# High and low part of x side by side: one 512-column matmul for both in the first feed-forward projections

## The chip, the cores and the metric
The kernel runs on one core of one Trainium2 chip. The metric is the device time of one execution in microseconds (us), the median over runs. TensorE (PE) multiplies, VectorE (DVE) and ScalarE (ACT) work elementwise, GpSimd (POOL) helps, and SyncE (SP) issues most DMAs. Matmul results land in PSUM, which has 8 banks of 512 fp32 values in each of 128 partitions; everything else on the chip lies in SBUF.

## The reference, cut to what matters
A sequence of 256 tokens of width 1024 goes through two blocks in fp32. The first has a mixer, attention over a memory and a feed-forward in each of two layers; the second has two layers of gated feed-forward, attention, gated feed-forward. The two kinds of feed-forward are

```python
def squared_relu_mlp(h, w1, w2):
    a = jax.nn.relu(h @ w1)
    return (a * a) @ w2

def swiglu(x, w_in, w_out):
    gate, up = jnp.split(x @ w_in, 2, axis=-1)
    return (jax.nn.silu(gate) * up) @ w_out
```

with 4096 inner columns in the first (two of them) and 2816 in the second (four of them). `h` is `x` after an RMS norm with a gain.

## The kernel before
Activations lie with the features on the partitions: x is 8 chunks of 128 features by 256 tokens. To keep fp32 accuracy every operand of a large matmul is split into a high part, which TensorE's fast fp32 format holds exactly, and a low part, the rest. A product is then three matmuls (`mm3`, L217 to L219): high weight by high x, low weight by high x, high weight by low x, each with 128x128 weights and 256 columns. The high and low part of x are the tiles `xhi` and `xlo`, written by `prep` (ACT for the high part, DVE for the low one); the gain is applied there, and the norm's factor for each token (`rstd_row`, whose matmul is L448) is applied when a result leaves PSUM.

Weights come in 568 groups of 128x1024. SP loads a group into one of the `raw` tiles, ACT rounds it into `rhi` (L204) and DVE subtracts for `rlo` (L242), each in halves of 512; seven groups are held split (`take`, `pump`, `split`).

A feed-forward loops over jobs. `W1(j)` takes a PSUM bank and two weight groups, runs `projs` (8 k-steps, two outputs of 256 columns side by side in the bank), and evicts the bank: in the gated one `evac_row` multiplies by the norm's factor (DVE L210), ACT applies silu, DVE multiplies, ACT and DVE split the result again. `W2` takes such a result as one chunk of the second projection (`rows`), which accumulates in banks 0 to 3 over the whole loop. `bank()` hands out banks 4 to 7 in turn; the stick stage (`stick_mixer`) hands out all 8.

The order of instructions on each engine is set by a list scheduler of the framework, which orders by priority and its own costs and then puts semaphore waits where one engine uses what another wrote or read. It tracks these dependences by tile. PSUM is eight tiles of one bank.

Attention stages (`even_mixer`, `mem_attention`, `band_mixer`, `stick_mixer`, `shared_kv`, `sink_mixer`) use the same banks: projections of q, k and v, scores, transposes and products, with VectorE and ScalarE between. In the stick stage each pair of heads has four matmuls into a bank A (L1224, L1226) and two into a bank B (L1228), whose sums DVE adds; in the sink stage a q projection is multiplied by the norm's factor and then rotated by a matmul (`rope`, L1245). During the first layer's memory attention, `mem_jobs` projects the memory; some of these jobs run later, as filler.

Of the kernel before, what the change touches and what calls it, by code (L numbers as in the profile page):

```python
# [8 lines left out]
F32 = mybir.dt.float32  # L9
# [92 lines left out]

class Kern:
    def __init__(self, nc, tc, ctx, d):
# [15 lines left out]
        self.xh = R(2048, "xhi")  # L120
        self.xl = R(2048, "xlo")
# [11 lines left out]
        self.psum = [ctx[1].tile([128, 512], F32, name=f"ps{i}") for i in range(8)]  # L133
# [131 lines left out]
    def proj(self, out, spec, xh=None, xl=None):  # L265
        xh = self.xh if xh is None else xh
        xl = self.xl if xl is None else xl
        wh, wl = self.take(spec)
        for k in range(8):
            self.mm3(out, wh[:, k * 128:(k + 1) * 128], wl[:, k * 128:(k + 1) * 128],  # L270
                     xh[:, k * 256:(k + 1) * 256], xl[:, k * 256:(k + 1) * 256], k == 0, k == 7)
        self.done()

    def projs(self, jobs, xh=None, xl=None):

        xh = self.xh if xh is None else xh
        xl = self.xl if xl is None else xl
        ws = [[self.take(spec) for spec in specs] for _, specs in jobs]
        for k in range(8):
            for (ps, _), w in zip(jobs, ws):  # L280
                for o, (wh, wl) in enumerate(w):
                    self.mm3(ps[:, o * 256:(o + 1) * 256], wh[:, k * 128:(k + 1) * 128], wl[:, k * 128:(k + 1) * 128],
                             xh[:, k * 256:(k + 1) * 256], xl[:, k * 256:(k + 1) * 256],
                             k == 0 and o == 0, k == 7 and o == len(w) - 1, skip=True)
        self.done(sum(len(w) for w in ws))

    def proj_toks(self, jobs, name, xh=None, xl=None):
        xh = self.xh if xh is None else xh
        xl = self.xl if xl is None else xl
        ws = [[self.take((name, "tok", c0, h)) for h in range(2)] for _, c0 in jobs]  # L290
        R = lambda z: z.bitcast(F32R)
        for k in range(8):
            for (ps, _), w in zip(jobs, ws):
                wh, wl = (R(z[:, (k % 4) * 256:(k % 4 + 1) * 256]) for z in w[k // 4])
                for t in range(2):
                    ah = R(xh[:, k * 256 + t * 128:k * 256 + (t + 1) * 128])
                    al = R(xl[:, k * 256 + t * 128:k * 256 + (t + 1) * 128])
# [6 lines left out]
    def proj_tok(self, ps, name, c0, xh=None, xl=None):  # L304
        self.proj_toks([(ps, c0)], name, xh, xl)

    def proj_wide(self, pss, name, c0, xh=None, xl=None):

        xh = self.xh if xh is None else xh
        xl = self.xl if xl is None else xl  # L310
        R = lambda z: z.bitcast(F32R)
        for q in range(4):
            wh, wl = self.take((name, "wide", c0, q))
            for k in (2 * q, 2 * q + 1):
                h, l = (R(z[:, (k % 2) * 512:(k % 2 + 1) * 512]) for z in (wh, wl))
                for t in range(2):
                    ah = R(xh[:, k * 256 + t * 128:k * 256 + (t + 1) * 128])
                    al = R(xl[:, k * 256 + t * 128:k * 256 + (t + 1) * 128])
# [34 lines left out]
    def prep(self, c, gain, x=None, xh=None, xl=None):  # L353
        x = self.x if x is None else x
# [146 lines left out]
    def mem_start(self, mem):  # L501
        for b in range(4):
            self.a.dma_start(mem[:, b * 512:(b + 1) * 512], self.d["mem"][:, b * 512:(b + 1) * 512])
        for b in range(4):
            for c in (2 * b, 2 * b + 1):
                self.prep(c, ("mg", 0), mem, self.mh, self.ml)
# [938 lines left out]
```

## Time and profile before

| | us |
|---|---|
| median of 3 runs | 1834.97 (1834.53 to 1837.04) |
| profiled execution, its own time | 1834.19 |
| its span | 1832.5 |
| TensorE busy | 1786.8 |
| VectorE busy | 1242.7 |
| ScalarE busy | 1033.3 |

The profiled execution is 1.7 us longer than its span, which begins with the first and ends with the last instruction. Busy times are sums over a stretch in which the engines overlap. A matmul's duration in a row is longer than the distance to the next matmul's start, since they are pipelined; the distance is what a matmul costs in a stream. TensorE's granted clock is full in nearly all of the span.

### The profile page before, as it was taken

How to read it: one execution, taken by the hardware profiler on the slowest of the kernel's cores; microseconds unless marked ns; L12 is line 12 of the kernel's file. 1: busy time of each engine (PE TensorE's matmuls, PEld its weight loads, DVE VectorE, ACT ScalarE, POOL GpSimd, SP SyncE). 2: the span in 40 equal slices, each digit the busy share in tenths (PEclk: the TensorE clock that was granted, in tenths of full speed). 3: DMA queues.
4: the chain of work that ended last, by engine and by line, in shares of the span. 5: the costliest groups of instructions: out<-in, count | busy, mean ns of one | idle time of the engine just before them, and what ended most of it. 6: DMA issues, size and time to landing. Idle time of an engine off the chain costs nothing.

```text
span 1832.5 us, 35979 instructions
## 1 busy us (share of the span) xinstructions
PE 1786.8 (98%) x14362; PEld 1741.3 (95%) x14362; DVE 1242.7 (68%) x2261; ACT 1033.3 (56%) x2037; POOL 110.3 (6%) x128
## 2 busy tenths in 40 slices
PE   7899999999999989998999999999999999999997
PEld 7889999999999989998999998999999999899997
DVE  7877786557687585557656778766586566876564
ACT  6556565556566465556444667644474455774443
POOL 2320000000000000000000002000010000200000
PEclk9999999999999999999999999999999999999999
DMA  7434445554653435553555553555545555335551
GB/s 272 159 119 137 161 148 198 185 184 156 225 166 139 156 133 189 187 185 137 188 190 176 184 173 127 172 174 188 191 162 187 181 181 174 118 128 188 192 173 35
DMA packets 85624, 307.80 MB, mean 168 GB/s; under 512 B 9680, under 2 KB 10320, under 8 KB 85456
## 3 DMA queue, kind: packets, MB, share of 16 engines
q1 hardware_dynamic: 83952, 300.92, 48.1%
q0 software_dynamic: 640, 3.15, 0.6%
q8 instruction: 112, 1.84, 0.4%
q10 hardware_dynamic: 864, 1.44, 0.2%
q14 instruction: 56, 0.46, 0.1%
HBM read 304.42 MB, written 1.05 MB: 167 GB/s over the span
## 4 chain that ended last, share of the span: by engine, by line
PE 92%; DVE 4%; ACT 2%; issue 1%; POOL 1%; DMA 0%; DVEq 0%; SPq 0%; ACTq 0%
PE ps L217 26%; PE ps L219 26%; PE ps L218 26%; PE ps L319 1%; PE ps L321 1%; PE ps L320 1%; DVE rlo L242 1%; PE ps L300 1%; PE ps L301 1%; PE ps L299 1%; PE ps L912 1%; PE ps L1080 1%; PE ps L930 1%; POOL u L210 1%; PE ps L448 1%
## 5 line engine op out<-in xcount | busy, mean ns | idle before, releaser
L204 ACT CAST rhi<-raw 128x512 fp32r<-128x512 f32 (+1 forms) x1138 | 669.8, 617 | 644.7 <-PE ps L219 609.3
L242 DVE TENSOR_TENSOR rlo<-raw,rhi 128x512 fp32r<-128x512 f32 (+1 forms) x1138 | 760.3, 693 | 342.0 <-ACT rhi L204 336.6
L217 PE MATMUL ps<-xhi,rhi 128*128 128x256 f32 x2560 | 732.5, 286 | 16.4 <-ACT xhi L192 9.5
L219 PE MATMUL ps<-xlo,rhi 128*128 128x256 f32 x2560 | 729.3, 285 | 4.3 <-DVE xlo L213 4.2
L218 PE MATMUL ps<-xhi,rlo 128*128 128x256 f32 x2560 | 729.3, 285 | 0.0
L217 PEld LDWEIGHTS ps<-xhi,rhi 128*128 128x128 f32 x2560 | 492.3, 192 | 18.9 <-ACT xhi L192 10.3
L219 PEld LDWEIGHTS ps<-xlo,rhi 128*128 128x128 f32 x2560 | 491.5, 192 | 6.5 <-DVE xlo L213 6.2
L218 PEld LDWEIGHTS ps<-xhi,rlo 128*128 128x128 f32 x2560 | 492.3, 192 | 0.7 <-DVE rlo L242 0.3
L217 PE MATMUL ps<-u,rhi 128*128 128x256 f32 x1680 | 474.6, 283 | 0.0
L219 PE MATMUL ps<-u,rhi 128*128 128x256 f32 x1680 | 471.8, 281 | 0.0
L218 PE MATMUL ps<-u,rlo 128*128 128x256 f32 x1680 | 471.4, 281 | 0.0
L217 PEld LDWEIGHTS ps<-u,rhi 128*128 128x128 f32 x1680 | 317.1, 189 | 0.9 <-issue 0.7
L218 PEld LDWEIGHTS ps<-u,rlo 128*128 128x128 f32 x1680 | 317.1, 189 | 0.4 <-issue 0.2
L219 PEld LDWEIGHTS ps<-u,rhi 128*128 128x128 f32 x1680 | 316.4, 188 | 0.7 <-DVE u L207 0.7
L210 DVE TENSOR_TENSOR u<-ps,rst 128x512 f32<-128x512 f32 (+1 forms) x129 | 84.1, 656 | 110.6 <-PE ps L219 110.2
L210 POOL TENSOR_TENSOR ssum<-ssum,sqb 128x512 f32<-128x512 f32 x26 | 38.0, 1461 | 1283.9 <-ACT sqb L192 1282.3
L192 ACT ACTIVATE u<-u 128x256 f32<-128x256 f32 (+3 forms) x158 | 86.2, 548 | 34.6 <-PE ps L702 17.1
L207 DVE TENSOR_TENSOR u<-u,u 128x256 fp32r<-128x256 f32 (+2 forms) x128 | 66.7, 521 | 10.2 <-ACT u L204 8.5
L204 ACT CAST u<-u 128x256 fp32r<-128x256 f32 (+2 forms) x128 | 61.9, 484 | 11.1 <-POOL u L1177 7.1
L213 DVE SCALAR_TENSOR_TENSOR xlo<-xres,gain,xhi 128x256 fp32r<-128x256 f32 x96 | 57.0, 620 | 3.1 <-ACT xhi L192 3.1
L192 ACT ACTIVATE xhi<-xres,gain 128x256 fp32r<-128x256 f32 x96 | 43.4, 501 | 26.4 <-DVE xres L210 19.7
L210 DVE TENSOR_TENSOR u<-u,u 128x256 f32<-128x256 f32 (+2 forms) x107 | 51.2, 481 | 0.6 <-ACT u L192 0.5
(170 smaller groups left out, 1261.2 us busy)
## 6 DMA issues: line engine op xcount, KB each, us to landing
raw<-w SPq DMA_DIRECT2D x567, 512.0 KB, 3.9
u<-bias POOLq DMA_DIRECT2D x8, 384.0 KB, 3.9
xres<-x SPq DMA_DIRECT2D x4, 256.0 KB, 5.3
u<-mem ACTq DMA_DIRECT2D x4, 256.0 KB, 4.0
raw<-w SPq DMA_DIRECT2D x2, 256.0 KB, 4.6
u<-tabs SPq DMA_DIRECT2D x1, 512.0 KB, 5.0
out<-u SPq DMA_DIRECT2D x2, 256.0 KB, 2.6
u<-masks SPq DMA_DIRECT2D x1, 256.0 KB, 6.4
```

The costliest lines, as they stand in the source:

```text
L192: i = self.a.activation(out, in_, func, scale=scale, **kw)
L204: return self.a.copy(out.bitcast(F32R), in_)
L207: return self.v.tensor_tensor(out.bitcast(F32R), in_, hi, ALU.subtract)
L210: return (eng or self.v).tensor_tensor(out, a, b, op)
L213: return self.v.scalar_tensor_tensor(out, a, s, b, op0, op1)
L217: self.pe.matmul(out, R(wh), R(xh), start=start, stop=False, skip_group_check=skip)
L218: self.pe.matmul(out, R(wl), R(xh), start=False, stop=False, skip_group_check=skip)
L219: self.pe.matmul(out, R(wh), R(xl), start=False, stop=stop, skip_group_check=skip)
L242: b = self.v.tensor_tensor(l[:, c].bitcast(F32R), r[:, c], h[:, c], ALU.subtract)
L299: self.pe.matmul(o, ah, wh, start=k == 0 and t == 0, stop=False, skip_group_check=True)
L300: self.pe.matmul(o, ah, wl, start=False, stop=False, skip_group_check=True)
L301: self.pe.matmul(o, al, wh, start=False, stop=k == 7 and t == 1, skip_group_check=True)
```

## The change
`xhi` and `xlo` become one tile `xpair`, in which each chunk has its 256 high columns and then its 256 low columns. `Pair` gives a chunk's both, high or low part; `Apart` gives the same for operands that stay in two tiles (the memory and the shared keys and values). All projections read x through them.

In W1 of both feed-forwards `projs2` takes the place of `projs`: for each k-step and output one matmul of the high weight with all 512 columns, into a whole bank, and one of the low weight with the 256 high columns, into the second half of the bank. So a job's two outputs take two banks, and each bank holds two partial sums. `halves` has ScalarE copy the second halves to SBUF and VectorE add the first ones; what followed then reads SBUF. PSUM is declared as four tiles of two banks; `psum[i]` are views of their halves, and `pair_bank` hands out the third and the fourth tile in turn. The row of sums in the feed-forwards uses bank 3.

```diff
+class Pair:
+    def both(self, c):
+        return self.tile[:, c * 512:(c + 1) * 512]
+    def h(self, c):
+        return self.tile[:, c * 512:c * 512 + 256]
+    def l(self, c):
+        return self.tile[:, c * 512 + 256:(c + 1) * 512]
...
-        self.xh = R(2048, "xhi")
-        self.xl = R(2048, "xlo")
+        self.xp = Pair(R(4112, "xpair")[:, 12:4108])
...
-        self.psum = [ctx[1].tile([128, 512], F32, name=f"ps{i}") for i in range(8)]
+        self.psum2 = [ctx[1].tile([128, 1024], F32, name=f"ps{i}") for i in range(4)]
+        self.psum = [self.psum2[i // 2][:, i % 2 * 512:(i % 2 + 1) * 512] for i in range(8)]
...
+    def pair_bank(self):
+        self.nbank += 3 - self.nbank % 2
+        return self.psum2[2 + self.nbank // 2 % 2]
+
+    def projs2(self, jobs):
+        ws = [[self.take(spec) for spec in specs] for _, specs in jobs]
+        R = lambda z: z.bitcast(F32R)
+        for k in range(8):
+            c = slice(k * 128, (k + 1) * 128)
+            for (ps, _), w in zip(jobs, ws):
+                for o, (wh, wl) in enumerate(w):
+                    self.pe.matmul(ps[:, o * 512:(o + 1) * 512], R(wh[:, c]), R(self.xp.both(k)),
+                                   start=k == 0, stop=False, skip_group_check=True)
+                    self.pe.matmul(ps[:, o * 512 + 256:(o + 1) * 512], R(wl[:, c]), R(self.xp.h(k)),
+                                   start=False, stop=k == 7, skip_group_check=True)
+        self.done(sum(len(w) for w in ws))
+
+    def halves(self, ps, low):
+        A, B = (ps.rearrange("p (a s b) -> p a s b", s=2, b=256)[:, :, i] for i in range(2))
+        self.act(self.two(low), B)
+        self.tt(self.two(low), self.two(low), A, ALU.add)
...
 # mlp
-            pss = [self.bank() for _ in js]
-            self.projs([(p, [("w_ff1", "col", l, (2 * j + o) * 128) for o in range(2)]) for p, j in zip(pss, js)])
+            pss = [self.pair_bank() for _ in js]
+            self.projs2([(p, [("w_ff1", "col", l, (2 * j + o) * 128) for o in range(2)]) for p, j in zip(pss, js)])
...
-                self.stt(self.two(t), self.two(ps), 0.0, self.row(st["r"], 2), ALU.max, ALU.mult)
+                self.halves(ps, t)
+                self.stt(self.two(t), self.two(t), 0.0, self.row(st["r"], 2), ALU.max, ALU.mult)
...
 # ffn
-            pss = [self.bank() for _ in js]
+            pss = [self.pair_bank() for _ in js]
...
-                self.projs([j])
+                self.projs2([j])
             if "r" not in st:
-                st["r"] = self.rstd_row()
+                st["r"] = self.rstd_row(self.psum[3])
...
-                self.evac_row(t, ps, st["r"])
+                self.halves(ps, t)
+                self.evac_row(t, t, st["r"])
```

The line numbers of the kernel after are some 30 to 50 higher: `mm3` is L249 to L251, the pair's matmuls are L329 (512 columns) and L331 (256), the row of sums is L495, `rope` is L1294, and L1224, L1226 and L1228 are L1273, L1275 and L1277.

The scheduler writes another order. Two places on TensorE, as the order of instructions gives them (line, operation, tile written, tiles read, columns, and the engine waited for). First the start of the sink stage, where the row of sums is followed by the first rope matmul. Before (`ps4` is one bank, as are the others):

```order
L218 MATMUL ps2_113<-xhi_89,rlo4_85 128x256
L448 MATMUL ps4_115<-ssum_91,tabs_66 128x256 [waits DVE_49]
L219 MATMUL ps2_113<-xlo_90,rhi4_78 128x256
...
L217 MATMUL ps6_117<-xhi_89,rhi6_80 128x256
L217 MATMUL ps4_115<-xhi_89,rhi5_79 128x256 [waits DVE_49]
L218 MATMUL ps4_115<-xhi_89,rlo5_86 128x256
...
L218 MATMUL ps6_117<-xhi_89,rlo6_87 128x256
L1245 MATMUL ps1_112<-u121_16265,u101_11968 128x256 [waits DVE_49]
L1245 MATMUL ps3_114<-u121_16265,u101_11968 128x256 [waits DVE_49]
```

After (`ps1` is two banks, as are the others):

```order
L251 MATMUL ps0_110<-xpair_89,rhi3_77 128x256 [waits DVE_49]
L495 MATMUL ps2_112<-ssum_90,tabs_66 128x256 [waits DVE_49]
L1294 MATMUL ps1_111<-u121_14888,u101_11207 128x256 [waits DVE_49]
L249 MATMUL ps1_111<-xpair_89,rhi4_78 128x256 [waits DVE_49]
L250 MATMUL ps1_111<-xpair_89,rlo4_85 128x256
...
L1294 MATMUL ps2_112<-u121_14888,u101_11207 128x256 [waits DVE_49]
L1144 MATMUL ps1_111<-u100_11206,u122_14889 128x256 [waits Pool_49]
```

Before, 42 projection matmuls stand between the row of sums and the first rope matmul; after, none does, and the next projection, in the other bank of the same tile, waits behind it.

Second a pair of heads in the stick stage. Before:

```order
L1224 MATMUL ps4_115<-u95_10804,exact_67 128x512 [waits DVE_49]
L1224 MATMUL ps4_115<-u98_10807,exact_67 128x512
L1226 MATMUL ps4_115<-u95_10804,exact_67 128x2x128
L1226 MATMUL ps4_115<-u98_10807,exact_67 128x2x128
L1228 MATMUL ps5_116<-u95_10804,exact_67 128x256 [waits DVE_49]
L1228 MATMUL ps5_116<-u98_10807,exact_67 128x256
L217 MATMUL ps6_117<-xhi_89,rhi0_74 128x256
```

After:

```order
L1273 MATMUL ps0_110<-u95_10043,exact_67 128x512 [waits DVE_49]
L1273 MATMUL ps0_110<-u98_10046,exact_67 128x512
L1275 MATMUL ps0_110<-u95_10043,exact_67 128x2x128
L1275 MATMUL ps0_110<-u98_10046,exact_67 128x2x128
L1245 MATMUL ps3_113<-u87_10035 128x128
L1277 MATMUL ps0_110<-u96_10044,exact_67 128x256 [waits DVE_49]
L1277 MATMUL ps0_110<-u99_10047,exact_67 128x256
L249 MATMUL ps0_110<-xpair_89,rhi2_76 128x256 [waits DVE_49]
```

The two banks A and B of one pair of heads no longer follow each other: the matmuls into B belong to the next pair of heads, lie beside the bank A that DVE reads, and wait for that read.

## Rows read from the trace of the kernel before

**Rows 1.** The page: busy times, and the chain that ended last by engine.
```profile
PE 1786.8 (98%) x14362; PEld 1741.3 (95%) x14362; DVE 1242.7 (68%) x2261; ACT 1033.3 (56%) x2037; POOL 110.3 (6%) x128
...
PE 92%; DVE 4%; ACT 2%; issue 1%; POOL 1%; DMA 0%; DVEq 0%; SPq 0%; ACTq 0%
```

**Rows 2.** The page's groups: line, engine, operation, count, busy and mean, idle before.
```profile
L217 PE MATMUL ps<-xhi,rhi 128*128 128x256 f32 x2560 | 732.5, 286 | 16.4 <-ACT xhi L192 9.5
```

**Rows 3.** Timeline of PE, 296 to 308 us: start, duration, line, operands.
```profile
295.94 0.28 PE L217 MATMUL ps<-xhi,rhi 128*128 128x256 f32 x1
...
301.69 0.28 PE L217 MATMUL ps<-u,rhi 128*128 128x256 f32 x1
...
307.33 0.28 PE L217 MATMUL ps<-xhi,rhi 128*128 128x256 f32 x1
```

**Rows 4.** Timeline of PE, 456 to 465 us: 36 matmuls of 512 columns.
```profile
456.76 0.39 PE L319 MATMUL ps<-rhi,xhi 128*128 128x512 f32 x1
...
464.71 0.39 PE L321 MATMUL ps<-rhi,xlo 128*128 128x512 f32 x1
```

**Rows 5.** Windows of one gated feed-forward round: length, busy time of each engine.
```profile
868.60:877.20 8.60, 8.60 (x75) 8.60 (x74) 5.15 (x9) 4.22 (x9) 0.00 (x0) 1.00 0.66 236
877.20:885.80 8.60, 8.60 (x75) 8.60 (x74) 5.15 (x9) 4.18 (x9) 0.00 (x0) 1.00 0.56 184
```

**Rows 6.** Groups by form: a PSUM copy on ACT, evictions and adds on DVE.
```profile
L192 ACT ACTIVATE u<-ps 128x512 f32<-128x512 f32 x11 | 6.6, 598 | 8.9 <-PE ps L921 8.2 <-PE ps L826 0.7
...
L210 DVE TENSOR_TENSOR u<-ps,rst 128x512 f32<-128x512 f32 x113 | 77.6, 690 | 110.4 <-PE ps L219 110.2
...
L210 DVE TENSOR_TENSOR u<-u,u 128x512 f32<-128x512 f32 x18 | 13.1, 742 | 0.1
```

**Rows 7.** Timeline, all engines, end of the first gated feed-forward.
```profile
1034.34 0.41 ACT L204 CAST u<-u 128x256 fp32r<-128x256 f32 x1
...
1034.78 0.43 DVE L207 TENSOR_TENSOR u<-u,u 128x256 fp32r<-128x256 f32 x1 [0.67 <-ACT u L204]
...
1035.03 0.28 PE L218 MATMUL ps<-u,rlo 128*128 128x256 f32 x1
1035.26 0.39 PE L219 MATMUL ps<-u,rhi 128*128 128x256 f32 x1
```

**Rows 8.** Timeline, all engines, start of the first gated feed-forward.
```profile
848.02 0.53 PE L217 MATMUL ps<-xhi,rhi 128*128 128x256 f32 x1 [4.76 <-ACT xhi L192]
...
848.47 0.47 DVE L213 SCALAR_TENSOR_TENSOR xlo<-xres,gain,xhi 128x256 fp32r<-128x256 f32 x1
```

**Rows 9.** Timeline, all engines, ahead of the first squared-relu feed-forward.
```profile
249.83 0.28 PE L217 MATMUL ps<-u,rhi 128*128 128x256 f32 x1
...
257.72 0.47 DVE L213 SCALAR_TENSOR_TENSOR xlo<-xres,gain,xhi 128x256 fp32r<-128x256 f32 x1
...
258.12 0.68 DVE L210 TENSOR_TENSOR u<-ps,mrst 128x512 f32<-128x512 f32 x1
...
266.98 0.59 PE L448 MATMUL ps<-ssum,tabs 128*128 128x256 f32 x2
```

**Rows 10.** Timeline, all engines, start of the sink stage.
```profile
1557.64 0.60 PE L448 MATMUL ps<-ssum,tabs 128*128 128x256 f32 x2
...
1562.67 0.75 DVE L210 TENSOR_TENSOR u<-ps,rst 128x256 f32<-128x256 f32 x2
...
1563.14 0.48 PE L1245 MATMUL ps<-u,u 128*128 128x256 f32 x1
```

**Rows 11.** Timeline, all engines, one pair of heads in the stick stage.
```profile
1098.45 0.40 PE L1226 MATMUL ps<-u,exact 128*128 128x256 f32 x2
1098.57 0.42 DVE L207 TENSOR_TENSOR u<-ps,u 128x256 fp32r<-128x256 f32 x1
1098.69 0.40 PE L1228 MATMUL ps<-u,exact 128*128 128x256 f32 x2
...
1099.50 0.68 DVE L210 TENSOR_TENSOR u<-u,ps 128x512 f32<-128x512 f32 x1
```

More of the change, by code (lines that the diff above doesn't have):

```diff
@@ L100, in __getitem__, with __init__, part, h @@
         return self.units[i][key[0], a - i * UNIT:b - i * UNIT]
+class Pair:
+    def __init__(self, tile):
+        self.tile = tile
+    def both(self, c):
[4 more added lines that the diff above has]
+        return self.tile[:, c * 512 + 256:(c + 1) * 512]
+    def part(self, c, n, i):
+        return self.tile[:, c * 512:(c + n) * 512].rearrange("p (a s b) -> p a s b", s=2, b=256)[:, :, i]
+class Apart:
+    def __init__(self, xh, xl):
+        self.xh, self.xl = xh, xl
+    def h(self, c):
+        return self.xh[:, c * 256:(c + 1) * 256]
+    def l(self, c):
+        return self.xl[:, c * 256:(c + 1) * 256]
 class Kern:
@@ L262, in pump, with proj, projs @@
             self.split()
[L265 to L267 removed]
+    def proj(self, out, spec, xp=None):
+        xp = xp or self.xp
         wh, wl = self.take(spec)
         for k in range(8):
[L270 to L271 removed]
+            self.mm3(out, wh[:, k * 128:(k + 1) * 128], wl[:, k * 128:(k + 1) * 128], xp.h(k), xp.l(k),
+                     k == 0, k == 7)
         self.done()
[L274 to L277 removed]
+    def projs(self, jobs, xp=None):
+        xp = xp or self.xp
         ws = [[self.take(spec) for spec in specs] for _, specs in jobs]
@@ L295, in proj_toks @@
                 for t in range(2):
[L296 to L297 removed]
+                    ah, al = (R(z(k)[:, t * 128:(t + 1) * 128]) for z in (xp.h, xp.l))
                     o = ps[:, t * 256:(t + 1) * 256]
@@ L351, in chunk, with prep @@
         return t[:, c * 256:(c + 1) * 256]
-    def prep(self, c, gain, x=None, xh=None, xl=None):
-        x = self.x if x is None else x
-        xh = self.xh if xh is None else xh
-        xl = self.xl if xl is None else xl
+    def prep(self, c, gain, x=None, xp=None):
+        x, xp = self.x if x is None else x, xp or self.xp
         g = self.gc(gain[0], gain[1] * 8 + c)
-        X, H, L = (self.chunk(t, c) for t in (x, xh, xl))
+        X, H, L = self.chunk(x, c), xp.h(c), xp.l(c)
         self.act(H.bitcast(F32R), X, AF.Identity, scale=g)
@@ L441, in rstd_spread, with rstd_row @@
         return out
-    def rstd_row(self):
-        ps = self.bank()
+    def rstd_row(self, ps=None):
+        ps = self.bank() if ps is None else ps
         zs = [z[:, i * 256:(i + 1) * 256] for z in self.sums for i in range(z.shape[-1] // 256)]
@@ L842, in even_mixer @@
             self.tt(sg[:, c], pso[j], sg[:, c], ALU.mult)
-            m = slice(1024 + j * 512, 1024 + (j + 1) * 512)
-            self.hi(mh[:, m], sg[:, c])
-            self.lo(ml[:, m], sg[:, c], mh[:, m])
-        ops = [(self.chunk(mh, c), self.chunk(ml, c)) for c in range(8)]
+            H, L = (mp.part(4 + 2 * j, 2, i) for i in range(2))
+            self.hi(H, self.two(sg[:, c]))
+            self.lo(L, self.two(sg[:, c]), H)
+        ops = [(mp.h(c), mp.l(c)) for c in range(8)]
         for c in range(6):
```

61 lines of the change are left out of this document (28 added, 33 removed).

## The prediction
> **What bounds the kernel now.** I read the page's busy times and its chain of waits first. TensorE is busy for 98% of the span and carries 92% of the chain that ends last [rows 1], so a microsecond taken from TensorE's stream of matmuls is a microsecond of the whole, and a wait put into that stream is one too. The grouped lines then say which matmuls: the 2560 triples on the normalised x are the largest block [rows 2], and 1920 of them are the first projections of the two squared-relu and the four gated feed-forwards (32 + 88 jobs, 16 k-steps each). The busy mean of 286 ns is no price, because matmuls overlap; the price is the distance from start to start in the timeline. There a triple on x runs from 295.94 to 301.69 us in 16 steps, 359.4 ns each, 119.8 ns per 256-column matmul; a triple on a feed-forward activation takes (307.33 - 301.69)/16 = 352.5 ns, 117.5 each [rows 3]. A 512-column matmul takes (464.71 - 456.76)/35 = 227.1 ns [rows 4]. Two 256s cost 239.6, so each matmul carries about 12.5 ns that do not grow with its columns. Last I read the windows of one feed-forward round: TensorE fills 8.60 of 8.60 us, VectorE 5.15, ScalarE 4.18 [rows 5].
>
> **The matmuls.** A triple of 359.4 ns becomes a pair of 227.1 + 119.8 = 346.9 ns: 12.5 x 1920 = 24.0 us less. The trace holds no 512-column matmul that streams x; the 227.1 rows stream weights. The one sign that a tile's place matters is x at 119.8 against activations at 117.5 [rows 3]. If the new x tile ran like the activations, the pair would be 342.3, the gain 17.1 x 1920 = 32.8, and the 640 triples that remain on x would give 6.9 x 640 = 4.4: 37 us in all. I take 24.0, the nearest row, with 37 as its other end. The Trainium skill, "TensorE: Matmul & The Clock Gate", section Back-to-back issue gap, gives a warm isolated gap of N/2.4 + 2.5 ns, and so 2.5 ns for each matmul saved: an estimate of 4.8 us instead of 24.0. The rows here stand at 119.8 and 227.1 where that rule gives 109.2 and 215.8; I follow the rows for the price and keep the rule as a rival.
>
> **The evictions.** Each job adds a ScalarE copy of 128x512 out of PSUM (598 ns) and a VectorE add of 128x512 (690 to 742 ns) [rows 6], 120 times each. In the steady rounds VectorE goes from 5.15 to about 5.9 and ScalarE from 4.18 to 4.8 us in a round that stays above 8.3 us [rows 5]; a pair of banks is wanted again a round later. I cost them at nothing there. If that cover were gone, each round would lose up to 1.34 us. Where a stage has no round to cover them they cost:
> At the four gated feed-forward ends the last W2 matmuls already wait: one starts at 1035.26 where its predecessor at 1035.03 asks for 1035.15, and the VectorE row that it needs ended at 1035.21 [rows 7]. Copy and add, 0.60 + 0.69, lengthen just this chain (with its table load), so 1.3 each, 5.2 in all.
> At the four gated starts the first matmul used to need only the high part: it starts at 848.02, while the low part is done at 848.47 + 0.47 = 848.94 [rows 8]. The 512-column matmul needs both, about 1.0 later, 4.0 in all.
> At the two squared-relu starts W1(0, 1) takes both pairs, so W1(2) waits for copy and add of the first: 1.2, and 1.0 more where the first W2 meets the longer chain: 2.2 each, 4.4.
> At the first of them a memory job also stands in the way. Before, two such jobs lay in two banks and the second started at 249.83, which covered the wait for x. Now both lie in one two-bank tile, and the second waits for the eviction of the first, which ends at 258.12 + 0.68 = 258.80 [rows 9]. The scheduler puts six k-steps of W1(0) ahead of it, each waiting on its low part, the sixth of which ends at 257.72 + 0.47 = 258.19 [rows 9]. Walking that order: six steps done at 258.9 (two more pairs), then 48 matmuls (5.6) and 20 pairs (6.9), 271.5 against 266.98 before [rows 9], so 4.5 late, and 4.9 against a stream that should have been 0.4 shorter. These four come to 18.5; I keep 10 and 22 as ends.
>
> **The tiles of two banks.** The change also makes PSUM four tiles of two banks for every stage. A wait is set per tile, so an instruction in one bank now waits for readers of the other. In the order of instructions, TensorE's waits on an instruction that touches only the neighbouring bank go from 14 to 171 (VectorE 118, ScalarE 53). Most are covered.
> The clearest is the start of the sink stage. After the row of sums L448 at 1557.64 TensorE ran 42 projection matmuls until the rope matmul L1245 at 1563.14 could start, whose VectorE row begins at 1562.67 [rows 10]. In the new order the rope matmul follows directly, because its bank's neighbour is the next projection's: 42 x 0.12 = 5.0 us of TensorE stand still, with 7 as the upper end since it also had other projections ahead.
> In the stick stage the two small matmuls L1228 followed L1226 at once (1098.45, 1098.69). They now lie beside the bank that VectorE reads in its add at 1099.50 + 0.68 = 1100.18 [rows 11], so up to 1.5 us per pair of heads; where other matmuls were scheduled between, nothing. A second wait, on the row L207 that ends at 1098.99 [rows 11], overlaps with it. I take 0.7 x 8 = 5.6 (ends 0 and 12). For the sink's other heads I take 0.4 x 8 = 3.2 (0 and 8), half the stick's price since there are shorter reads; for the band 0.2 x 8 = 1.6 (0 and 4); for row tails, memory attention and the first mixer 2.1 (0 and 5). Sum 17.5, ends 5 and 36.
>
> **The sum** is -24.0 + 18.5 + 17.5 = +12.0. It is made against the profiled execution, 1834.2 us (span 1832.5 and 1.7 outside); the median of the runs lies 0.8 higher, so 1834.97 + 12.0 = 1847.
>
> **Rivals.** First, faster: the waits on the neighbouring bank stay hidden but for the sink's start, and x in its new place runs at the activations' price. Place: the stick, sink and band stages and every pair. Price: -37 + 15 + 5 = -17, 1818 us. For it: the scheduler saw these waits and put other matmuls before most of them, and VectorE is busy only 68% [rows 1]. Against it: TensorE is in order and full there, and the sink's start shows 42 covering matmuls moved away. It decides where waits and starts together cost less than the pairs give, 24 to 37 us.
> Second, a draw: pairs at the middle price, -30, starts 18, waits 10: -2, 1833 us. Nothing in the trace speaks against it but that each cost would come out low.
> Third, more clearly slower: the fixed part of a matmul's price sits in the columns or in the weight load and not in the instruction, so a pair with the same columns costs a triple's 359.4 ns: 0 + 18.5 + 17.5 = +36, 1871 us. Place: every one of the 1920 pairs; it decides as soon as a pair costs over 353 ns, half of the gain gone. Against it: 227.1 stands against 2 x 119.8 in rows of this trace [rows 3, 4]. By the rule of the Trainium skill, "TensorE: Matmul & The Clock Gate", Back-to-back issue gap, which leaves an estimate of 4.8 us of gain, it would be 1866 us; the trace does not agree with that rule's prices.
>
> **How the numbers follow.** Chances: the forecast 0.55, the first rival 0.24, the draw 0.13, the third 0.08. A measurement of this kernel can tell about 0.2%, 3.7 us, from no change. So slower is 0.63, within 0.2% 0.13, faster 0.24. The ends of the terms added give 1835 - 37 + 10 + 5 = 1813 and 1835 - 24 + 22 + 36 = 1869; both at once are unlikely, and 1820 to 1866 leaves out part of the first rival and the third.
>
> **What would show it.** In the profile after, the pairs start to start: 347 ns, or 342. The gated round: 8.57 becomes about 8.37. TensorE's idle time before the sink's rope matmul: 5 us, waiting for VectorE. Idle on TensorE in front of the small stick matmuls: about 0.7 each. The first squared-relu sum row: some 4.5 later than now. The forecast is wrong if TensorE's idle in the attention stages grows by less than 8 us in sum, or if the pairs run below 342 ns.

## The result and the profile after

The changed kernel takes 1915.01 us (1913.39 to 1917.25), the kernel before 1835.12 us in the same comparison. The ratio is 1.0434, with a 95% interval of 1.0416 to 1.0452: 80 us slower, where 12 us were forecast. The sign was right, the time lies far outside the range. The page's busy times and clock, answering to [rows 1], and the two kinds of matmul that take the place of [rows 2]:

```profile
PE 1823.1 (95%) x12442; PEld 1665.6 (87%) x12442; DVE 1320.0 (69%) x2381; ACT 1094.0 (57%) x2157; POOL 108.5 (6%) x128
...
PEclk9999999999999989998999998999999999899998
...
L329 PE MATMUL ps<-xpair,rhi 128*128 128x512 f32 x1920 | 687.2, 399 | 16.0 <-DVE xpair L245 14.5
L331 PE MATMUL ps<-xpair,rlo 128*128 128x256 f32 x1920 | 540.9, 282 | 0.0
```

TensorE has 1920 matmuls fewer and is busy 36.3 us longer (1823.1 against 1786.8). Its idle time grew from 45.7 to 90.1 us (span 1913.2 less busy). So nearly half of the loss is not in the idle column at all. The mean granted clock fell from 0.994 to 0.975.

The pairs did what was said of them, at first. The timeline of TensorE at the place of [rows 3]:

```profile
299.81 0.40 PE L329 MATMUL ps<-xpair,rhi 128*128 128x512 f32 x1
300.04 0.28 PE L331 MATMUL ps<-xpair,rlo 128*128 128x256 f32 x1
...
303.97 0.40 PE L329 MATMUL ps<-xpair,rhi 128*128 128x512 f32 x1
```

From 299.81 to 303.97 lie 12 pairs, 346.7 ns each; forecast were 346.9. But over the rounds of the first gated feed-forward (some 280 pairs) the mean distance is 232.7 + 118.4 = 351.1 ns, where the triples stood at 359.6.

The waits of TensorE by line waited for (sum in us, times, longest):

```profile
PE ps L329 <- DVE xpair L245: 14.5, 7, 5.1
PE ps L495 <- DVE ssum L242: 7.7, 4, 2.4
PE ps L249 <- ACT u L236: 7.3, 5, 1.9
PE ps L1294 <- DVE u L242: 7.1, 4, 4.3
...
PE ps L959 <- DVE u L242: 4.9, 2, 4.2
...
PE ps L1277 <- DVE u L242: 3.3, 3, 1.6
```

L329 is the start of a feed-forward, which now needs both parts of x ([rows 8] before). L1294 is the sink stage's rope matmul and L1277 the stick stage's small matmul, the two places shown in the order of instructions. TensorE at the sink's start, answering to [rows 10]:

```profile
1622.26 0.32 PE L251 MATMUL ps<-xpair,rhi 128*128 128x256 f32 x1
1623.74 0.70 PE L495 MATMUL ps<-ssum,tabs 128*128 128x256 f32 x2 [1.15 <-DVE ssum L242]
1628.73 1.22 PE L1294 MATMUL ps<-u,u 128*128 128x256 f32 x2 [4.30 <-DVE u L242]
1630.47 0.58 PE L249 MATMUL ps<-xpair,rhi 128*128 128x256 f32 x1 [0.52 <-DVE u L242]
1630.85 0.41 PE L250 MATMUL ps<-xpair,rlo 128*128 128x256 f32 x1
```

Nothing covers the wait: 4.30 us, and then two matmuls start 0.38 us apart. In the stick stage (all engines; [rows 11]) the small matmul waits for the add that reads the neighbouring bank, and further on the same pattern ends in half-speed matmuls:

```profile
1137.38 0.40 PE L1275 MATMUL ps<-u,exact 128*128 128x256 f32 x2
...
1137.81 0.69 DVE L242 TENSOR_TENSOR u<-u,ps 128x512 f32<-128x512 f32 x1
...
1138.65 0.47 PE L1277 MATMUL ps<-u,exact 128*128 128x256 f32 x2 [0.87 <-DVE u L242]
...
1153.58 0.51 PE L1277 MATMUL ps<-u,exact 128*128 128x256 f32 x2 [1.65 <-DVE u L242]
```

Windows of the stick stage (length; busy time and count of PE, PEld, DVE, ACT, POOL; granted clock; DMA share; GB/s):

```profile
1110.00:1130.00 20.00, 19.75 (x149) 18.25 (x148) 12.84 (x25) 12.82 (x22) 1.21 (x2) 1.00 0.49 158
1130.00:1150.00 20.00, 18.15 (x119) 15.75 (x119) 13.03 (x25) 11.56 (x18) 3.35 (x7) 0.91 0.26 80
1150.00:1170.00 20.00, 16.99 (x79) 13.77 (x79) 10.44 (x21) 8.98 (x15) 3.15 (x6) 0.74 0.23 79
1170.00:1190.00 20.00, 19.15 (x121) 16.39 (x122) 10.65 (x19) 11.31 (x18) 3.68 (x6) 0.91 0.25 80
```

TensorE starts 79 matmuls in 20 us instead of 149. It looks 85% busy all the same: a matmul in this interrupted stream is booked as busy for 0.4 to 0.6 us where it costs 0.12 in a full one, and at a mean clock of 0.74 TensorE had its half level for half of the stretch.

**Where the 80 us arise.** The matmuls of the second projections and the last writes of x in each stage, which both kernels have, were laid side by side and their delay noted (worked out from both timelines, in us). The delay is 8 when x is written ahead of the first squared-relu feed-forward, 14 in its first rounds and 13 in its last, 23 after the band stage, 33 when x is written ahead of the second squared-relu feed-forward, 35 in its first rounds and 34 in its last, 37 ahead of the first gated one, 38 in its first rounds, 35 in its last and 37 behind it. The stick stage adds 26 (64). The second gated one ends at 63; the shared keys and values add 4 (67), and the third gated one ends at 66. The sink's start adds 12 (78) and its heads some 3 (81); the last feed-forward takes 2 back. So some 70 us come from the attention stages, where the change altered the tiles of PSUM and the place of x, and some 8 from the six feed-forwards. Within their rounds these give back some 12 us (1 in each squared-relu one, 2.4 in each gated one); their starts and ends cost more than that.

### The profile page after: what moved, and what is told of

Read it like the earlier page. It is cut to its first block, busy times and chain, and to the rows that moved or that the text cites. A ratio compares the mean times of both kernels' runs of the same rounds, so it can differ in the third digit from the quotient of the medians.

```text
span 1913.2 us, 32338 instructions
## 1 busy us (share of the span) xinstructions
PE 1823.1 (95%) x12442; PEld 1665.6 (87%) x12442; DVE 1320.0 (69%) x2381; ACT 1094.0 (57%) x2157; POOL 108.5 (6%) x128
## 5 line engine op out<-in xcount | busy, mean ns | idle before, releaser
L236 ACT CAST rhi<-raw 128x512 fp32r<-128x512 f32 (+1 forms) x1138 | 678.2, 616 | 527.0 <-PE ps L329 312.2
L329 PE MATMUL ps<-xpair,rhi 128*128 128x512 f32 x1920 | 687.2, 399 | 16.0 <-DVE xpair L245 14.5
L331 PE MATMUL ps<-xpair,rlo 128*128 128x256 f32 x1920 | 540.9, 282 | 0.0
L249 PE MATMUL ps<-u,rhi 128*128 128x256 f32 x1680 | 478.2, 285 | 8.0 <-ACT u L236 7.3
L251 PE MATMUL ps<-u,rhi 128*128 128x256 f32 x1680 | 471.8, 282 | 0.6 <-DVE u L245 0.3
L329 PEld LDWEIGHTS ps<-xpair,rhi 128*128 128x128 f32 x1920 | 364.4, 190 | 102.0 <-DVE xpair L245 19.0
L331 PEld LDWEIGHTS ps<-xpair,rlo 128*128 128x128 f32 x1920 | 365.7, 190 | 0.3
L249 PEld LDWEIGHTS ps<-u,rhi 128*128 128x128 f32 x1680 | 317.4, 189 | 19.4 <-ACT u L236 9.0
L251 PEld LDWEIGHTS ps<-u,rhi 128*128 128x128 f32 x1680 | 316.0, 189 | 1.5 <-DVE u L239 0.7
L249 PE MATMUL ps<-xpair,rhi 128*128 128x256 f32 x640 | 189.3, 296 | 10.9 <-ACT rhi L236 7.1
L251 PE MATMUL ps<-xpair,rhi 128*128 128x256 f32 x640 | 187.0, 292 | 4.5 <-DVE xpair L245 4.4
L250 PE MATMUL ps<-xpair,rlo 128*128 128x256 f32 x640 | 186.2, 291 | 0.1
L249 PEld LDWEIGHTS ps<-xpair,rhi 128*128 128x128 f32 x640 | 126.2, 197 | 15.4 <-ACT rhi L236 7.1
L251 PEld LDWEIGHTS ps<-xpair,rhi 128*128 128x128 f32 x640 | 125.8, 197 | 6.7 <-DVE xpair L245 5.8
L250 PEld LDWEIGHTS ps<-xpair,rlo 128*128 128x128 f32 x640 | 126.2, 197 | 0.8 <-DVE rlo L274 0.5
L224 ACT ACTIVATE u<-ps 128x512 f32<-128x512 f32 (+1 forms) x179 | 100.4, 564 | 30.9 <-PE ps L1245 10.7
L242 DVE TENSOR_TENSOR u<-u,ps 128x512 f32<-128x512 f32 (+2 forms) x152 | 98.2, 652 | 8.5 <-ACT u L224 5.0
```

Of the source, the lines that this page charges most:

```text
L224: i = self.a.activation(out, in_, func, scale=scale, **kw)
L236: return self.a.copy(out.bitcast(F32R), in_)
L242: return (eng or self.v).tensor_tensor(out, a, b, op)
L249: self.pe.matmul(out, R(wh), R(xh), start=start, stop=False, skip_group_check=skip)
L250: self.pe.matmul(out, R(wl), R(xh), start=False, stop=False, skip_group_check=skip)
L251: self.pe.matmul(out, R(wh), R(xl), start=False, stop=stop, skip_group_check=skip)
```

## The experiments

Theory A, the main one: the two-bank tiles cost most of it, in the attention stages. Its rivals put the loss on the pairs, on the starts and ends of the feed-forwards, or on where the new x tile lies.

**Only the tiles.** The kernel before with PSUM as four two-bank tiles and nothing else:

```diff
-        self.psum = [ctx[1].tile([128, 512], F32, name=f"ps{i}") for i in range(8)]
+        self.psum2 = [ctx[1].tile([128, 1024], F32, name=f"ps{i}") for i in range(4)]
+        self.psum = [self.psum2[i // 2][:, i % 2 * 512:(i % 2 + 1) * 512] for i in range(8)]
```

> The kernel before with one edit: PSUM declared as four tiles of two banks, its eight banks views of them. No matmul and no eviction changes. Theory A (the tiles of two banks cost most of the 80 us, through waits on the neighbouring bank in the attention stages): 45 to 70 us slower than before, with most of it in the stick stage (20 to 30), the sink stage (10 to 18), the band (4 to 8) and the memory attentions. Theory B (the loss is in the feed-forwards, in starts, ends and the pair's own price): within 10 us of before.

Measured: 1903.82 us, ratio 1.0381 (1.0364 to 1.0398): 69 us more, with the same matmuls. The sum is as theory A had it; the stick stage, given 20 to 30, is not. Its delays: 14 up to the first squared-relu start, 8 more in the band, 8 to the second squared-relu start, 2 at a gated start, 12 to 14 in the stick stage, 7 in the shared keys and values, 13 in the sink stage, and none in any feed-forward round. Its page:

```profile
PE 1826.9 (96%) x14362; PEld 1760.2 (93%) x14362; DVE 1253.0 (66%) x2261; ACT 1035.0 (54%) x2037; POOL 109.7 (6%) x128
```

TensorE is busy 40.1 us longer for the very same 14362 matmuls, at a mean clock of 0.989, and idle 28.5 us longer (74.2 against 45.7). The same stretch of the band stage in the kernel before,

```profile
487.50:562.50 75.00, 74.44 (x629) 69.29 (x628) 56.62 (x133) 45.78 (x125) 3.22 (x6) 1.00 0.53 166
```

and in the kernel with only the tiles:

```profile
503.70:586.70 83.00, 81.81 (x634) 72.98 (x633) 57.96 (x133) 47.48 (x127) 3.22 (x6) 1.00 0.48 150
```

Same work, full clock in both, 8.0 us longer, and 7.4 of these are booked as busy. By the distances between starts, 28 more matmuls than before stand 0.20 to 0.35 us apart, where most stand 0.12 apart; hardly one gap is longer than 0.45 us. The list of waits shows almost nothing of it. What it is, the part on company below takes up.

**Everything but the tiles.** The changed kernel with eight one-bank tiles; `halves` copies and adds each bank by itself, as 256 columns:

```diff
-        self.psum2 = [ctx[1].tile([128, 1024], F32, name=f"ps{i}") for i in range(4)]
-        self.psum = [self.psum2[i // 2][:, i % 2 * 512:(i % 2 + 1) * 512] for i in range(8)]
+        self.psum = [ctx[1].tile([128, 512], F32, name=f"ps{i}") for i in range(8)]
...
-        return self.psum2[2 + self.nbank // 2 % 2]
+        i = 4 + 2 * (self.nbank // 2 % 2)
+        return self.psum[i:i + 2]
```

> The kernel after with PSUM as eight tiles of one bank again; a pair is two such tiles, and the eviction is two copies and two adds of 256 columns in place of one each of 512. Theory A: 55 to 75 us faster than the kernel after, so 1840 to 1860, with the attention stages back at their length of before. Theory B: 5 to 10 us slower than the kernel after, since the eviction has two more instructions.

Measured: 1833.32 us, ratio 0.9992 (0.9983 to 1.0001), 82 us less than the changed kernel, more than the 55 to 75 expected. The delays of the attention stages are gone. What is left, by the matmuls of the second projections: +3.4 and +5.4 at the two squared-relu starts, -1.6 at the four gated ones together (their first pairs already save), -11.6 in the rounds of all six feed-forwards, and +2.5 at each of the first three gated ends and 0.3 at the last.

The elementwise instructions on a job's result stand some 2 us later still in the rounds, since copy and add lengthen their chain. They come back at the end of each feed-forward, and TensorE, which sets the time, does not wait for them in the rounds; a delay read from them makes a start look some 2 us too dear.

The second squared-relu start, as TensorE's timeline has it (start, duration, and the idle time before), first in the kernel before and then in this one:

```profile
657.05 0.58 PE L217 MATMUL ps<-xhi,rhi 128*128 128x256 f32 x1 [4.76 <-ACT xhi L192]
```

```profile
653.68 1.13 PE L497 MATMUL ps<-sqb,tabs 128*128 128x256 f32 x4
660.54 0.80 PE L329 MATMUL ps<-xpair,rhi 128*128 128x512 f32 x1 [5.73 <-DVE xpair L244]
...
682.69 0.39 PE L248 MATMUL ps<-u,rhi 128*128 128x256 f32 x1 [1.80 <-ACT u L235]
```

and a window of this one:

```profile
660.00:665.00 5.00, 4.46 (x14) 3.78 (x15) 5.00 (x10) 3.30 (x7) 1.90 (x2) 0.50 0.01 4
```

The wait is 1 us longer, since the first matmul now needs both parts of x. In it the granted clock falls to its half level, 1.2 GHz, where it stands for 6.8 us in this kernel and for 3.4 us in the one before; 14 matmuls fill 5 us. The first matmul of the second projection then waits 1.80 us for the longer chain.

**The place of the x tile.** The changed kernel with x at value 0, and at value 8, of its tile instead of 12:

```diff
-        self.xp = Pair(R(4112, "xpair")[:, 12:4108])
+        self.xp = Pair(R(4112, "xpair")[:, 0:4096])
```

> The kernel after with the x tile at its start (offset 0 in place of 12 values). Theory P (the place of x in SBUF sets the price of a 512-column matmul: 232.7 ns here against 227.1 in the kernel before, whose x tiles lie at offset 0): 512 columns at 227, 256 columns at 120, a pair 347 in place of 351, 6 to 9 us faster than the kernel after. Rival (the price is of the pattern, not of the place): pair at 351, same time.

> The kernel after with the x tile at offset 8 values, where the activations' tiles lie in the kernel before (117.5 ns for 256 columns there). Theory P: 512 columns at 225 to 227, 256 at 117.5, a pair 342 to 345, 11 to 18 us faster than the kernel after. Rival: pair at 351, same time.

Measured: 1910.29 us (1.0408, 1.0393 to 1.0424) and 1906.90 us (1.0390, 1.0375 to 1.0406), 4.7 and 8.1 less than the changed kernel; 6 to 9 and 11 to 18 were expected. A pair costs 231.1 + 115.8 = 346.9 and 228.9 + 118.1 = 347.1 ns, against 351.1 at value 12; neither 227 ns for 512 columns nor a pair of 345 ns came out at any place. So the place sets the price, by up to 4 ns for a pair. It is a small part of the 80 us.

**The place alone, without pairs.** The kernel before, `xhi` and `xlo` each begun 8 values into a tile that is 16 values wider, which also moves every tile behind them:

```diff
-        self.xh = R(2048, "xhi")
-        self.xl = R(2048, "xlo")
+        self.xh = R(2064, "xhi")[:, 8:2056]
+        self.xl = R(2064, "xlo")[:, 8:2056]
```

> The kernel before with one edit: xhi and xlo begin 8 values (32 bytes) into tiles of 2064. No instruction is added or removed. Theory P (the place of an operand in SBUF sets the price): the 256-column matmuls on x fall from 120 to 117.5 or 118 ns, 7680 of them, 15 to 19 us faster than before, about 1818. Rival (the place matters only for 512-column matmuls): within 3 us of before.

Measured: 1818.23 us, ratio 0.9906 (0.9891 to 0.9921): 16 us for nothing but addresses, with TensorE's matmuls in the same order. A matmul on x costs 117.5 to 118.6 ns where it cost 119.8 to 120.0, one on an activation 116.5 to 117.3 instead of 117.4 to 118.3 (means over the first gated feed-forward).

**The starts and the ends.** First the one-bank kernel with x at value 8 and the first W1 of each feed-forward as triples (core of the edit):

```diff
-            pss = [self.pair_bank() for _ in js]
+            pair = js[0] > 0
+            pss = [self.pair_bank() if pair else self.bank() for _ in js]
```

Then, added to it, the last W1 of the gated ones as triples too:

```diff
-            pair = js[0] > 0
+            pair = 0 < js[0] < NFF - 1
```

> The run with one-bank tiles (e2), x at offset 8, and the first W1 of each feed-forward (jobs 0 and 1 of the squared-relu ones, job 0 of the gated ones) as triples in one bank each, evicted as before. Theory C (in e2 the two squared-relu starts cost 7 and 9 us, since the first two jobs take all four banks and every matmul needs both parts of x): these two starts come back to 0 to 2 us behind before, and with the place of x (7 to 8 us) the whole is 18 to 24 us faster than e2, 1809 to 1815. Rival (the starts lose to the clock, which falls in the wait of 5 us that stands there in any case): only the place is gained, 1824 to 1827.

> As e6, and the last W1 of each gated feed-forward as triples too. Theory C: the four ends get back the copy and the add in the chain of the last job, 1.3 us each at most (e2 shows 0.7 to 1.1), so 3 to 5 us faster than e6. Rival (the end is set by another wait, so the chain is covered): within 1 us of e6.

Measured: 1819.72 us (0.9919, 0.9904 to 0.9933), 13.6 less than with one-bank tiles alone, and 1813.15 us (0.9883, 0.9868 to 0.9897), 6.6 less again. The first is short of the 18 to 24 us expected, though the two squared-relu starts are back (0.6 and 0.3 us in the matmuls of the second projections): the 7 and 9 us expected from them are the delay of the first elementwise instructions on the jobs' results (6.9 and 9.3), and on TensorE they had cost 3.4 and 5.4. The second is more than the 3 to 5 expected: 1.65 us for each gated end in the mean.

**Which banks share a tile.** The changed kernel with the count of banks moved on by one at the start of the stick stage:

```diff
     def stick_mixer(self, g2):
+        self.nbank += 1
         self.lowbanks = True
```

> The kernel after with one edit: the count that hands out banks is one higher at the start of the stick stage, so the two banks of a pair of heads lie in one tile and not in the tiles of two pairs of heads. Theory N (what a neighbouring bank costs depends on whose work shares the tile: the stick stage loses 26 us in the kernel after and 12 in the run e1, where the count stands differently): the stick stage loses 10 to 16 us, the whole is 10 to 16 us faster than the kernel after, about 1902. Rival (the stick stage loses more in the kernel after because of its own reads of x or of the clock): within 4 us of the kernel after.

Measured: 1900.87 us (1.0360, 1.0342 to 1.0377), 14 less than the changed kernel; the stick stage adds 11 us instead of 26. What two-bank tiles cost depends on which two uses meet in one tile.

**More triples, and another place for the activations.** From the kernel with first and last W1 as triples: a tile for x wider by 16 values, which moves the activations; then the jobs 2 and 3 of the squared-relu ones as triples too:

```diff
-        self.xp = Pair(R(4112, "xpair")[:, 8:4104])
+        self.xp = Pair(R(4128, "xpair")[:, 8:4104])
...
-            pair = 0 not in js
+            pair = js[0] > 3
```

> As e7, with the x tile 64 bytes longer behind its end (4128 values), which moves the activations' tiles behind it by 64 bytes and nothing else. Theory P: the 256-column matmuls on activations, 118.2 ns in e7 and 116.7 in e5, where they lie at this place, fall to 116.7 to 117; 5040 of them in the second projections and the output projections, 5 to 8 us faster than e7, about 1806. Rival (118.2 comes from the pairs before them, not from the place): within 2 us of e7.

> As e10, and jobs 2 and 3 of the squared-relu feed-forwards as triples too. Theory C (the first pairs stall because their banks are still being evicted while nothing else is ready): the two starts, which lie 3 us behind before in e7, come back by 1 to 3 us each, 2 to 5 us faster than e10. Rival (the 3 us are the clock after the wait of 5 us, which stands in before as well): within 2 us of e10, or slower by the pairs given up, 64 of them at 5 ns.

Measured: 1806.88 us (0.9847, 0.9832 to 0.9862) and 1807.33 us (0.9851, 0.9834 to 0.9867). The place gives 6.3 us more, the further triples nothing: the 3 us which they were to win back stood in the chain of the jobs' results, and TensorE's matmuls had lost 0.9 and 0.0 us at these two starts. 1806.88 is the best version here, 28 us under the kernel before and 108 under the changed one.

**Half of the tiles.** The kernel before with banks 4 to 7 as two two-bank tiles, banks 0 to 3 single:

```diff
+        two = lambda z: [z[:, 0:512], z[:, 512:1024]]
-        self.psum = [ctx[1].tile([128, 512], F32, name=f"ps{i}") for i in range(8)]
+        self.psum = [ctx[1].tile([128, 512], F32, name=f"ps{i}") for i in range(4)]
+        for i in (4, 6):
+            self.psum += two(ctx[1].tile([128, 1024], F32, name=f"ps{i}"))
```

> The kernel before with banks 4 to 7 as two tiles of two banks, which is all that the pairs need, and banks 0 to 3, where the second projections accumulate, as tiles of one bank. Theory H (most of the 69 us of e1 come from the banks that are handed out in turn, 4 to 7, in the attention stages; the accumulators add the row tails and half of the stick stage): 40 to 60 us slower than before. Rival (the accumulators' banks cost most, since every second projection ends in them and the next stage's first projections reuse them): under 30 us slower than before.

Measured: 1879.45 us (1.0243, 1.0226 to 1.0260): 44.5 of the 69 us. The banks 4 to 7 are what the change needed as pairs; the other 24 us it paid for four banks of which no pair is ever handed out.

**Company: matmuls of two heads side by side.** What are the 40 us of busy time? The scores of two heads (`pair_scores`) are matmuls of 64 rows, one head in partitions 0 to 63, the other in 64 to 127, fp32, each in two records. Groups of such matmuls by form in the kernel before (L1195 and L1196 are the stick stage's; "ps<-u,u" is the sink, "ps<-u" the band):

```profile
L1195 PE MATMUL ps<-u 64*128 64x256 f32 x32 | 6.4, 428 | 0.0
L1095 PE MATMUL ps<-u,u 64*128 64x256 f32 x32 | 6.4, 428 | 0.6 <-POOL u L210 0.6
L1095 PE MATMUL ps<-u 64*128 64x256 f32 x32 | 5.7, 428 | 0.0
...
L1096 PE MATMUL ps<-u 64*128 64x128 f32 x32 | 3.2, 270 | 0.0
```

and in the kernel with only the tiles:

```profile
L1096 PE MATMUL ps<-u 64*128 64x256 f32 x32 | 9.1, 428 | 0.1
L1096 PE MATMUL ps<-u,u 64*128 64x256 f32 x32 | 9.1, 427 | 0.1
L1196 PE MATMUL ps<-u 64*128 64x256 f32 x32 | 8.1, 476 | 0.5 <-DVE u L208 0.5
...
L1097 PE MATMUL ps<-u 64*128 64x128 f32 x32 | 5.1, 274 | 0.0
```

The same count and the same mean, but 9.1 us instead of 5.7: busy time is counted once where instructions overlap, and they overlap less. Before, the two heads start 14 ns apart. This row of before holds four records of L1095, two for each head:

```profile
491.08 0.71 PE L1095 MATMUL ps<-u 64*128 64x256 f32 x4
491.61 0.40 PE L1096 MATMUL ps<-u 64*128 64x128 f32 x4
491.94 0.39 PE L217 MATMUL ps<-xhi,rhi 128*128 128x256 f32 x1
```

and with only the tiles one head takes as long alone:

```profile
527.35 0.70 PE L1096 MATMUL ps<-u 64*128 64x256 f32 x2
527.89 0.38 PE L1097 MATMUL ps<-u 64*128 64x128 f32 x2
528.20 0.39 PE L219 MATMUL ps<-xhi,rlo 128*128 128x256 f32 x1
```

0.86 us for two heads before, 0.85 us for one now. Starts less than 40 ns apart fall from 232 in the kernel before to 153 with only the tiles; in the changed kernel they are also 153, in the one with one-bank tiles 241. The scheduler pulls the heads apart: with one-bank tiles the four matmuls of two heads follow each other in the order of instructions; with two-bank tiles, where the second head's bank lies in another tile, it puts other work between, for five of the eight pairs in the band and five in the sink, where it was none and one before (in the third pair of the band, the second head's first matmul stands 67 records behind the first head's). In the stretch of the band shown above, the groups with 64 rows or 64 columns take 5.7 of the 7.4 us booked as busy. Summed over the eight groups of scores and products of heads with 64 rows or 64 columns, TensorE is busy 57.4 us before, 76.5 with only the tiles, 79.3 after the change, and 56.4 with one-bank tiles. The Trainium skill, "TensorEngine Tiling (Array Packing)", Key Properties, says that different tiles of the array can run matmuls in parallel; these rows agree.

Two runs put a price on it. One has the tiles, and makes both heads use one tile:

```diff
     def pair_scores(self, q, k):
         out = []
+        self.nbank += 1 - self.nbank % 2
```

The other has the kernel before and its tiles, and sets a 16-column matmul of all 128 rows between the heads:

```diff
             ps = self.abank()
+            if e:
+                self.pe.matmul(ps[:, 384:400], self.tb("ident"), self.tb("ident")[:, 0:16], start=True, stop=True)
             self.pe.matmul(ps[:, 0:256], qe[:, 128:256], ke, start=True, stop=True)
```

> The kernel before with four two-bank tiles, as in the run with only the tiles, but the scores of a pair of heads (band and sink stage) always take the two banks of one tile. Theory S (part of what the tiles cost is that the 64-row score matmuls of two heads no longer start side by side, because the scheduler sets the second head's apart when its bank lies in another tile): in the order the two heads' matmuls follow each other again, starts of matmuls less than 40 ns apart go from 153 to 175 or more (232 before the tiles), and the time falls by 8 to 14 us against 1903.8, to 1890 to 1896. Rival (only waits matter, the company does not): the starts come back, the time stays within 4 us of 1903.8.

> The kernel before, banks as they were, with one added matmul of 16 columns that uses all 128 rows between the two heads' score matmuls of the band and sink stages (its result is overwritten), so that the heads cannot run side by side; no wait is added. Theory S: 16 pairs of heads lose each other's company, 0.86 us each by the trace of before (eight records in 0.86 us at 491.08, which is what one head alone takes in the kernel with only the tiles, 527.35 to 528.20), 13.7 us, and 2 to 4 us for the added matmuls: 1848 to 1853. Rival (the company is worth nothing): only the added matmuls, 1837 to 1839.

Measured: 1850.34 us for the heads kept apart (1.0081, 1.0064 to 1.0097), 15.5 us more than before for 16 pairs of heads, the added matmuls included. In its trace the added matmuls hold TensorE for 5.0 us, 325 ns each with two exceptions:

```profile
492.60 0.38 PE L1098 MATMUL ps<-u 64*128 64x128 f32 x2
492.90 0.40 PE L1096 MATMUL ps<-tabs 128*128 128x16 f32 x2
493.23 0.70 PE L1097 MATMUL ps<-u 64*128 64x256 f32 x2
```

So by this the company is worth some 10 us of the 15.5, 0.66 us a pair, where 0.86 was expected; that the total came out as expected is in part luck. The groups of the band and the sink, 6.4 and 5.7 us before, in this kernel:

```profile
L1097 PE MATMUL ps<-u,u 64*128 64x256 f32 x32 | 11.1, 428 | 0.6 <-POOL u L210 0.6
L1097 PE MATMUL ps<-u 64*128 64x256 f32 x32 | 11.1, 428 | 0.0
```

But 1900.87 us for the tiles with both heads in one (1.0357, 1.0342 to 1.0373), only 3 less than with only the tiles, as the rival had it. The starts came back (197), and the same groups with them:

```profile
L1097 PE MATMUL ps<-u,u 64*128 64x256 f32 x32 | 6.4, 427 | 0.0
L1097 PE MATMUL ps<-u 64*128 64x256 f32 x32 | 5.7, 428 | 0.0
```

TensorE's busy time falls by 5.7 us, and its idle time grows by 4.9 (74.2 to 79.0): the band stage adds 4 us instead of 8 and the sink 10 instead of 13, while the stick and the shared keys and values add more than they did. So the lost company is real where nothing else changes, but with two-bank tiles the order that restores it waits elsewhere: giving it back to these heads does not give the time back. In the run with the count of banks moved by one it came with the time: TensorE is busy 10.7 us less than in the changed kernel (1812.4 against 1823.1), 9 of it in these eight groups, and idle 2.9 us less. Of the 69 us, 28.5 are idle time and 19 are busy time in these groups; how the other 21 us of busy time divide between short waits, a poorer interleaving and the half clock was not separated.

## Why the prediction was right or wrong

**The step that failed: the tiles of two banks.** It had 17.5 us, with ends of 5 and 36; alone they cost 69 us, and on top of the one-bank version 82. "Most are covered" was the wrong sentence. Of the 171 waits on a neighbouring bank, the text priced those that it could name in the order and gave the rest almost nothing. By place, forecast against measured (only the tiles; after the change): the sink's start 5.0 against 3 to 4; 12. The sink's rest 3.2 against 9; 3. The stick 5.6 against 12 to 14; 26. The band 1.6 against 8; 6. Row tails, memory attention and first mixer 2.1, against 17; 20 ahead of the second squared-relu feed-forward, without the band and the first feed-forward; the shared keys and values, which had no price at all, 7; 4. The mechanism named for the sink and the stick is in the trace of after, row for row (4.30, 0.87 and 1.65 us). The places called small had 6.9 us, and with the shared keys and values came to 41 with only the tiles and 33 after the change.

Three things were missing. A scheduler that sees the longer dependences writes another order, and that order lost the company of 64-row matmuls; the order had already shown it, but was read for its waits alone. A row's wait was taken as its whole price, though TensorE then runs at the half level for some microseconds: the mean clock of 0.975 instead of 0.994, spread over the span, is some 70 us more at that level (2 x (1 - clock) x span: 96 against 22). Some of that is idle time, so the matmuls lost less. At the half level a 256-column matmul stands at 214 ns (118 to 120 at full) and one of 512 columns at 426 (233); the changed kernel has 165 and 32 of them there, the kernel before 59 and none, which makes an estimate of 16 us. And the neighbours in a tile are set by a counter of banks, so the stick's price moved by 14 us with one step of it: no row of the trace could have told that price without the order.

**The pairs: right mechanism, wrong size.** A pair of 346.9 ns was forecast; 346.9 and 347.1 stand at values 0 and 8 of the tile, 346.7 in the first rounds after the change, but 351.1 over the first gated feed-forward. That the sum came out at value 0 is luck: its terms were 227.1 and 119.8, and 231.1 and 115.8 were measured. The sign given, "x at 119.8 against activations at 117.5", pointed at the right thing, that the place matters; which way the new place would go was not to be seen, and the other end, 342 ns, came out nowhere. A triple of 359.6 that becomes a pair of 351.1 gives 8.5 x 1920 = 16.3 us, where 24.0 were forecast. The third rival, that a pair saves nothing, is out.

The rule quoted with it from the Trainium skill, "TensorE: Matmul & The Clock Gate", Back-to-back issue gap, is an isolated gap of N/2.4 + 2.5 ns. The prediction's estimate from it, 2.5 ns for each matmul saved, does not fit these rows: 8.5 to 12.7 ns were saved.

**Starts and ends: about right in the changed kernel.** Forecast 18.5. From the last write of x to the matmuls of the second projection, the first squared-relu start adds 5.8 us (8.4 to 14.2), where 2.2 and 4.9 stood, and its sum row comes 4.9 later than x (13.3 less 8.4), as worked out; the second adds 2.4, where 2.2 stood. The three gated starts that can be read by themselves add 0.7, -0.4 and -0.4, first pairs included, where 1.0 each stood; the four gated ends 2.0, 2.1, 2.1 and 1.0, together 7.2, where 5.2 stood. With one-bank tiles, where the 4.9 for the memory job has no cause, the squared-relu starts cost 3.4 and 5.4 against 2.2 each: at the second the sum left out the wait for the low part of x (5.73 us instead of 4.76) and the longer half clock.

**Evictions at no cost in the rounds: right.** In the rounds of no feed-forward does the delay of TensorE's matmuls grow, in any of these kernels. The forecast that the gated round falls from 8.57 to 8.37 holds in direction: 16 pairs at 351.1 and 24 matmuls at 118.4 make 8.46.

**The sign and the rivals.** Slower had 0.63, and it is slower. The faster rival needed the tiles' waits to stay hidden; with one-bank tiles the change is a draw (0.9992), and with the place and the starts mended it is faster (0.9847). Against the place alone without pairs (1818.23) the pairs are then worth some 11 us, of which part may be another place again.

## What to carry to other kernels

When an edit changes the size of a tracked tile, compare the whole order of instructions on the full engine, stage by stage, also for what no longer stands together; here a price for "other places" taken from the named ones was far too low. Declare as wide tiles only what is used as such: here one-bank tiles with two copies and two adds gave the same pairs 82 us cheaper. And do not read a stage's loss from idle time alone: in the band the same matmuls were booked 7.4 us longer as busy, at full clock, and 5.7 of it was lost overlap. Read a delay from the engine that sets the time: the chain of the jobs' results was 2 us later, and TensorE did not wait for it.

## What the runs showed of the hardware

The 64-row matmuls of two heads, in the two halves of the partitions, start 14 ns apart and take together what those of one head take alone: 0.86 against 0.85 us. Keeping them apart cost 15.5 us for 16 pairs of heads, of which the matmuls that kept them apart hold 5.0.

The place of the streamed operand in SBUF sets a matmul's price. With x at value 0, 8 and 12 of its tile, a 512-column matmul stood at 231.1, 228.9 and 232.7 ns, and the 256-column one behind it at 115.8, 118.1 and 118.4. With x and what lies behind it moved by a few dozen bytes, a 256-column matmul on x went from some 119.9 to between 117.5 and 118.6, which gave the kernel before 16 us. What the rule of it is, these runs don't tell.

Waits on TensorE came with matmuls at the half level of the clock: 0.50 from 660 to 665 us, at the end of the wait of 5.73 us and behind it, in the one-bank kernel, and 0.74 over 20 us of the stick stage, where waits of 0.5 to 1.65 us follow each other. At that level a 256-column matmul stood at 214 ns where it costs 118 to 120 at the full one.
